# Hybrid mLSTM and short-convolution block: opening, gate arithmetic, maxima broadcast and tail in another form

## Chip, cores and metric

The kernel runs on one core of a Trainium2 chip. The metric is device time of one execution in microseconds, the median of several runs. TensorE (PE) multiplies matrices, VectorE (DVE) and ScalarE (ACT) do elementwise work, GpSimd (POOL) a little of it, SyncE (SP) issues the DMAs. Each engine runs its own instructions in order; between engines they wait on semaphores.

## The reference

One decoder layer on x (256 tokens, 2048 features), float32 throughout. What is computed:

```python
mod = silu(c) @ w_ada + b_ada                      # shift, scale, gate
h = rms_norm(x, norm1_w) * (1 + scale) + shift
proj = h @ w_in + b_in       # q k v o z | i f | u B C z_b | gA gB
h_a = mlstm(q, k, v, i, f)                         # 8 heads, running max m as stabiliser
h_a = rms_norm(sigmoid(o) * h_a, headnorm_w) * silu(z)
h_b = B * causal_conv3(C * u) * silu(z_b)
merged = sigmoid(gA) * (h_a @ w_proj_a) + sigmoid(gB) * (h_b @ w_proj_b)
out = rms_norm(x + gate * (merged @ w_out), normf_w)
```

## The kernel before

**Units.** All weights are streamed once in units of 128x1024 float32 (512 KB), in the order of the list that `units()` yields: "outer" units (q/k, v, o, z, gA: one block of 128 rows of w_in and half of a group's columns, accumulated over 16 row blocks k), two "if" units for the gates, "inner" units (gB, u, C, B, zb, yA, yB: a block j of 512 output columns, eight units each), and "out" units (w_out: row block k, half of the columns). SP loads a unit into `raw`, up to six ahead. ACT copies it into a rounded head `wh` (L302), DVE subtracts that for the remainder `wl` (L308), and TensorE multiplies three times: head by head, remainder by head, head by remainder. A unit is 12 matmuls of 512 columns or 24 of 256. The loop over UNITS first splits the unit two places ahead (`advance`), then issues this unit's matmuls, then runs one entry of the list `fillers`: the list by which everything that is not a weight matmul is dealt out between the units. The order on each engine is the order of the code.

**Opening (L127 to L280).** xT (x transposed, four DMAs) and the row c are loaded. c goes into row 0 of a zeroed tile `c_row`, and four matmuls with ones (L207) spread it over the partitions for Silu (`silu_c`, tile c_b). ACT squares xT in four pieces, DVE adds some of them, and matmuls with ones (L221) sum them over the features; the outcome stands on all partitions, 256 tokens wide, so that rstd_b is its root (L236) and reciprocal (L266) over 128x256. `keep_warm(n)` issues n matmuls on ones (L198) whose result nobody reads: `WARM[0]` at the start, `WARM[1]` behind the sums. The columns of w_ada come as pieces (part 1 scale, 0 shift, 2 gate; row block k; half) which DVE multiplies with c_b and sums (L261). After the fourth piece of block k, xT is scaled (L271) and h is made as head on ACT (L255) and remainder on DVE (L256). The first weight matmul is L333 of q/k.

**Gates.** `gates_rows` takes the i and f rows (8 heads by 256 tokens) out of PSUM beside gB block 0. `gates_math` is four fillers, `one` to `four` (L523 to L550): log-sigmoid, running sum, running maximum, and the negated maximum `mrow` as head and remainder, each 8x256. `gates_cols` (L553) turns two of the rows into columns with four transposes. Then three fillers a head follow each other (`queue_mlstm`): `stage_a` (scores, and the head's row of `mrow` spread over 128 partitions by two matmuls with 8 rows, L574 and L575), `stage_b1` to `b3` (decay matrix), `stage_c` (values), `stage_d`, and after all heads `stage_e`, `stage_y` and the transposes `stage_t`.

**Tail (from L984).** The out units accumulate into cur[t, half], t being the two tiles of 128 tokens. The split weights of the last KEEP = 4 row blocks are kept in keepH and keepL: the loop over them completes t = 0 alone, with the halves alternating, and afterwards the TAIL list completes t = 1 in six pieces of 512 or 256 columns (L1003). `out_evac` multiplies each piece by the gate (L854) and adds x (L855) on DVE, squares with a sum on ACT (L861), and multiplies by normf_w on POOL (L863). `out_root` takes the root, `out_finish` scales chunks of 512 columns (L895 on DVE, L897 on ACT; the last one, L893, with the weights on DVE) and SP sends them out.

Of the kernel before, what the change touches and what calls it, by code (L numbers as in the profile page):

```python
# [45 lines left out]
KEEP = 4  # L46
WARM = (9, 16)
# [4 lines left out]
def units():  # L52
# [43 lines left out]
def body(ctx: ExitStack, tc: tile.TileContext, wu, wa, xT_d, x_d, cols_d, rows_d, out_d):  # L96
# [32 lines left out]
    c_row = slot("s3", [128, D], "c_row")  # L129
    dve.memset(ones, 1.0)  # L130
    dve.memset(c_row[:, 0:1024], 0.0)
    pool.memset(c_row[:, 1024:2048], 0.0)
    dve.memset(dummy, 1.0)
# [9 lines left out]
    identr = slot("identr", [NH, NH], "identr", F32R)  # L143
# [3 lines left out]
    pieces = [(part, k, half) for k in range(16) for part in (1, 0) for half in range(2)]  # L147
# [60 lines left out]
    ssq = psum("a", "ssq")[:, 0, 0:S]  # L208
# [49 lines left out]
    def ada_piece(n):  # L258
# [6 lines left out]
        if n == 2:  # L265
            dve.reciprocal(rstd_b, rstd_b)  # L266
        if part == 0 and half == 1:
            a, b = ab[:, 0, k:k + 1], ab[:, 1, k:k + 1]
            dve.scalar_tensor_tensor(a, acc[:, 1, k, 0:1], bs1[:, k:k + 1], acc[:, 1, k, 1:2], op0=ALU.add, op1=ALU.add)
            dve.tensor_tensor(a, a, col("n1", k), op=ALU.mult)  # L270
            dve.scalar_tensor_tensor(xT[:, k, :], xT[:, k, :], a, rstd_b, op0=ALU.mult, op1=ALU.mult)  # L271
            dve.scalar_tensor_tensor(b, acc[:, 0, k, 0:1], col("b_shift", k), acc[:, 0, k, 1:2], op0=ALU.add, op1=ALU.add)
            blocks.append((state["now"], k))
            if k == 0:
                split_head(0, 0)
                make_h(0)
                split_head(0, 1)
# [240 lines left out]

    def gates_math():
# [557 lines left out]
```

## Time and profile before

| what | us |
|---|---|
| median of three runs | 1154.69 (1153.08 to 1155.09) |
| profiled execution, its own time | 1153.19 |
| its span, first to last instruction | 1151.4 |
| PE busy in the span | 1134.3 |
| DVE busy | 832.9 |
| ACT busy | 573.4 |

The profile is one execution. Its span is 1.8 us shorter than its time: that is what lies around the first and last instruction. The page gives busy times and the costliest groups; the timeline lists instructions in order of time, rows of equal ones merged, with the idle time before them and what ended it; the chain of waits goes back from the last instruction to what released each. A matmul's length in the timeline contains the time it takes to drain through the array, so the rate is read from starts, or from the length of a long row divided by its count.

### The profile page before, as it was taken

What the parts mean: (1) busy time and instruction counts of PE and PEld (TensorE: products, weight loads), DVE (VectorE), ACT (ScalarE), POOL (GpSimd) and SP (SyncE); (2) the same over time, 40 slices, a digit from 0 to 9 for tenths busy, and PEclk for the clock granted to TensorE, in tenths of its full rate; (3) what the DMA queues carried; (4) which work ended last, traced back from release to release, by engine and by line L of the source; (5) the groups of instructions that cost most, each with busy time, mean ns of one, the idle gap of its engine ahead of it and who ended that gap; (6) DMA issues with size and microseconds to landing.
All of it is one profiled execution on the core that took longest, in us unless ns stands there. A gap on an engine that the chain in (4) does not pass through costs nothing.

```text
span 1151.4 us, 16498 instructions
## 1 busy us (share of the span) xinstructions
PE 1134.3 (99%) x6402; PEld 1021.1 (89%) x6402; DVE 832.9 (72%) x1016; ACT 573.4 (50%) x668; POOL 16.5 (1%) x26
## 2 busy tenths in 40 slices
PE   8999999999999999999999999999999999999996
PEld 7888899988888888888999999999999888888885
DVE  6999998999888768667587666666666655555566
ACT  6764444464454546544547644544544444443453
POOL 0000000000000000000000000000000000000003
PEclk9999999999999999999999999999999999999999
DMA  9999999999888767644468676666665766487662
GB/s 345 390 387 373 338 334 348 374 376 364 319 293 312 231 217 262 201 161 151 150 190 277 189 207 206 191 210 203 194 206 194 212 197 196 145 294 234 204 201 74
DMA packets 80464, 286.41 MB, mean 249 GB/s; under 512 B 10753, under 2 KB 10881, under 8 KB 79745
## 3 DMA queue, kind: packets, MB, share of 16 engines
q1 hardware_dynamic: 80386, 285.36, 73.0%
q8 instruction: 50, 0.82, 0.3%
q14 instruction: 28, 0.23, 0.1%
HBM read 283.22 MB, written 2.11 MB: 248 GB/s over the span
## 4 chain that ended last, share of the span: by engine, by line
PE 92%; DVE 4%; ACT 2%; issue 1%; DMA 0%; DVEq 0%; SPq 0%; ACTq 0%
PE qk L333 7%; PE v L364 7%; PE z L364 7%; PE gA L364 7%; PE o L364 6%; PE out L364 6%; PE u0g L333 2%; PE C0g L333 2%; PE B0g L333 2%; PE gB1g L356 2%; PE gB2g L356 2%; PE gB3g L356 2%; PE yA3g L356 2%; PE yA0g L356 2%; PE yA2g L356 2%; PE yA1g L356 2%
## 5 line engine op out<-in xcount | busy, mean ns | idle before, releaser
L308 DVE TENSOR_TENSOR wl<-raw,wh 128x1024 fp32r<-128x1024 f32 x408 | 496.7, 1222 | 255.4 <-ACT wh L302 253.8
L302 ACT ACTIVATE wh<-raw 128x1024 fp32r<-128x1024 f32 x409 | 430.0, 1058 | 440.9 <-PE v L364 39.2
L261 DVE SCALAR_TENSOR_TENSOR ada<-ada,c_b 128x1024 f32<-128x1024 f32 x96 | 116.9, 1218 | 1.3 <-DMA ada<-wa 1.3
L364 PE MATMUL o<-wh,h 128*128 128x512 f32 x256 | 66.5, 380 | 0.6 <-DVE z L413 0.4
L364 PE MATMUL v<-wh,h 128*128 128x512 f32 x256 | 66.4, 379 | 0.0
L364 PE MATMUL z<-wh,h 128*128 128x512 f32 x256 | 66.0, 379 | 0.0
L364 PE MATMUL gA<-wh,h 128*128 128x512 f32 x256 | 66.0, 379 | 0.0
L333 PE MATMUL qk<-h,wh 128*128 128x256 f32 x512 | 62.7, 276 | 1.4 <-ACT h L255 1.4
L333 PEld LDWEIGHTS qk<-h,wh 128*128 128x128 f32 x512 | 60.0, 192 | 1.7 <-ACT h L255 1.6
L364 PEld LDWEIGHTS o<-wh,h 128*128 128x128 f32 x256 | 48.2, 189 | 8.2 <-issue 0.8
L364 PEld LDWEIGHTS v<-wh,h 128*128 128x128 f32 x256 | 48.2, 189 | 7.1 <-issue 0.4
L364 PEld LDWEIGHTS gA<-wh,h 128*128 128x128 f32 x256 | 48.4, 189 | 6.8
L364 PEld LDWEIGHTS z<-wh,h 128*128 128x128 f32 x256 | 48.3, 189 | 6.8
L364 PE MATMUL out<-wh,m 128*128 128x512 f32 x192 | 49.7, 379 | 0.0
L364 PEld LDWEIGHTS out<-wh,m 128*128 128x128 f32 x192 | 36.1, 189 | 5.1
L364 PE MATMUL v<-wl,h 128*128 128x512 f32 x128 | 38.1, 379 | 0.0
L364 PE MATMUL o<-wl,h 128*128 128x512 f32 x128 | 38.1, 379 | 0.0
L364 PE MATMUL z<-wl,h 128*128 128x512 f32 x128 | 38.1, 379 | 0.0
L364 PE MATMUL gA<-wl,h 128*128 128x512 f32 x128 | 38.1, 379 | 0.0
L333 PE MATMUL qk<-h,wl 128*128 128x256 f32 x256 | 33.8, 275 | 0.0
L333 PEld LDWEIGHTS qk<-h,wl 128*128 128x128 f32 x256 | 31.2, 192 | 0.0
L364 PE MATMUL out<-wl,m 128*128 128x512 f32 x96 | 28.6, 379 | 0.0
(430 smaller groups left out, 2114.2 us busy)
## 6 DMA issues: line engine op xcount, KB each, us to landing
raw<-wu SPq DMA_DIRECT2D x418, 512.0 KB, 4.4
ada<-wa SPq DMA_DIRECT2D x96, 512.0 KB, 6.3
xT<-xT SPq DMA_DIRECT2D x4, 512.0 KB, 6.1
gB<-rows SPq DMA_DIRECT2D x2, 1024.0 KB, 5.8
x_res<-x SPq DMA_DIRECT2D x1, 2048.0 KB, 8.0
out<-r SPq DMA_DIRECT2D x8, 256.0 KB, 2.6
gA<-rows SPq DMA_DIRECT2D x2, 512.0 KB, 7.5
z<-rows SPq DMA_DIRECT2D x2, 512.0 KB, 7.7
```

What stands on the lines that cost most here:

```text
L261: dve.scalar_tensor_tensor(t, t, 1.0, c_b[:, half * 1024:half * 1024 + 1024], op0=ALU.mult, op1=ALU.mult, accum_out=acc[:, part, k, half:h ...
L302: act.activation(head[n], r, AF.Copy)
L308: dve.tensor_tensor(rest[n], r, head[n].bitcast(F32), op=ALU.subtract)
L333: pe.matmul(o, lhsT=w[:, j + 128 * b:j + 128 * b + 128], rhs=alt(h[:, k, :]), start=st and b % 2 == 0, stop=en and b % 2 == 1, skip_group_ ...
L356: pe.matmul(o[:, t, :], lhsT=stationary(a, k, t), rhs=alt(ww[:, c0:c0 + 512]), start=st, stop=en, skip_group_check=True)
L364: pe.matmul(o[:, b, :], lhsT=stationary(a, k, t), rhs=alt(ww[:, c0 + 512 * b:c0 + 512 * b + 512]), start=st, stop=en, skip_group_check=True)
```

## The change

**Opening.** c is loaded first of all into a tile of its own, c_in, and copied into c_row, its left half by DVE and its right half by ACT. The squares are summed with tokens on the partitions: the square is the stationary operand, ones are streamed, so that `ssq` is 128x2 columns of use. Root and reciprocal work on 128x2 (`rs`). `x_norm` scales the identity by rs (two tiles dg on ACT) and spreads it with two matmuls (`rb`), which the first block's scaling reads from PSUM; ACT copies it to rstd_b for the others. The first four pieces of w_ada come as half 0 of both parts, then half 1. The warming matmuls are 6, 2, 16 and 12 in four places.

**Gates and maxima.** `gates_math` is seven fillers, and one idle filler goes, so the heads start two units later. The head and the remainder of the maxima stand in one tile of 40 partitions (0 to 7 and 32 to 39, zeros between, prepared at unit 60 by `pick_prepare`); `pick(h)` makes a 40x128 selector on ACT, and one matmul with 40 rows spreads both. One idle filler before the last transpose goes.

**Tail.** The last four row blocks of the out units come as half 0 of all four and then half 1. All splits left are issued at once behind the first of them. The first token tile's four chunks are scaled on ACT, one piece of the TAIL list earlier than before; of the second tile's chunks DVE scales 0 and 3, ACT 1 and 2, and ACT issues the DMA of chunk 2.

```diff
-WARM = (9, 16)
+WARM = (6, 2, 16, 12)
-    for k0, k1 in ((0, 4),) + tuple((k, k + 1) for k in range(4, 16)):
+    for k0, k1 in ((0, 4),) + tuple((k, k + 1) for k in range(4, 16 - KEEP)) + ((16 - KEEP, 16),):
...
+    c_in = slot("s01", [1, D], "c_in")
+    sync.dma_start(c_in, rows_d[ROWS.index("c"):ROWS.index("c") + 1, :])
...
-        if i == 0:
-            sync.dma_start(c_row[0:1, :], rows_d[ROWS.index("c"):ROWS.index("c") + 1, :])
+    dve.tensor_copy(c_row[0:1, 0:1024], c_in[:, 0:1024])
+    act.activation(c_row[0:1, 1024:2048], c_in[:, 1024:2048], AF.Copy)
...
-    pieces = [(part, k, half) for k in range(16) for part in (1, 0) for half in range(2)]
+    pieces = [(part, 0, half) for half in range(2) for part in (1, 0)]
+    pieces += [(part, k, half) for k in range(1, 16) for part in (1, 0) for half in range(2)]
...
-            pe.matmul(ssq, lhsT=ones, rhs=sq[:, b, :], start=first and b == 0, stop=last and b == n - 1)
+            for t in range(2):
+                pe.matmul(ssq[:, t, 0:128], lhsT=sq[:, b, 128 * t:128 * t + 128], rhs=ones, start=first and b == 0,
+                          stop=last and b == n - 1)
...
+    keep_warm(WARM[1])
     square(0)
+    silu_c(0)
     square(1)
-    silu_c(0)
-    dve.tensor_tensor(sqs[0], sqs[0], sqs[1], op=ALU.add)
-    dve.tensor_tensor(sqs[0][:, 0:2, :], sqs[0][:, 0:2, :], sqs[0][:, 2:4, :], op=ALU.add)
-    sum_squares(sqs[0][:, 0:2, :], True, False)
     square(2)
-    sum_squares(sqs[2], False, False)
+    dve.tensor_tensor(sqs[2][:, 0:2, :], sqs[2][:, 0:2, :], sqs[2][:, 2:4, :], op=ALU.add)
     square(3)
+    silu_c(1)
+    sum_squares(sqs[0], True, False)
+    sum_squares(sqs[1], False, False)
+    sum_squares(sqs[2][:, 0:2, :], False, False)
     sum_squares(sqs[3], False, True)
-    silu_c(1)
     act.activation(dummy, ones[:, 0:1], AF.Sqrt)
+    rs = slot("rs", [128, 2, 1], "rs")
+    act.activation(rs, ssq[:, :, 0:1], AF.Sqrt, bias=eps_c, scale=1.0 / D)
+    keep_warm(WARM[2])
...
-    act.activation(rstd_b, ssq, AF.Sqrt, bias=eps_c, scale=1.0 / D)
-    act.activation(identr, ident[0:NH, 0:NH], AF.Copy)
-    keep_warm(WARM[1])
+    def x_norm():
+        dve.reciprocal(rs, rs)
+        for t in range(2):
+            dg = wp.tile([128, 128], F32, name=f"dg{t}", tag="dmat", bufs=2)
+            act.activation(dg, ident, AF.Copy, scale=rs[:, t, :])
+            pe.matmul(rb[:, 0, 128 * t:128 * t + 128], lhsT=ones, rhs=dg, start=(t == 0), stop=(t == 1),
+                      skip_group_check=True)
+        keep_warm(WARM[3])
...
         if n == 2:
-            dve.reciprocal(rstd_b, rstd_b)
+            x_norm()
+            scale()
+            split_head(0, 0)
+            split_head(0, 1)
...
+    def pick(h):
+        ml["pick", h] = wp.tile([32 + NH, 128], F32R, name=f"pick{h}", tag="pick", bufs=2)
+        act.activation(ml["pick", h], ones[0:32 + NH, :], AF.Copy, scale=ml["sel"][:, h:h + 1])
...
-        return [one, two, three, four]
+        return [one, two, three, four, five, six, seven]
...
-        pick = identr[:, h:h + 1].to_broadcast([NH, 128])
-        pe.matmul(p[:, 1, 0:256], lhsT=pick, rhs=ml["mr"][0], start=True, stop=False)
-        pe.matmul(p[:, 1, 0:256], lhsT=pick, rhs=ml["mr"][1], start=False, stop=True)
+        pe.matmul(p[:, 1, 0:256], lhsT=ml["pick", h], rhs=ml["mr"], start=True, stop=True)
...
-        fillers.extend([idle, idle, gates_cols])
+        fillers.extend([idle, gates_cols])
...
-            fillers.append(heads((stage_b2, i - 1), (stage_d, i - 3), (stage_b3, i - 1)))
+            fillers.append(heads((stage_b2, i - 1), (stage_d, i - 3), (stage_b3, i - 1), (pick, i + 1)))
...
-            elif c % 2 == 0:
+            elif t and c == 0:
                 dve.tensor_scalar(r, r, tot, None, op0=ALU.mult)
             else:
                 act.activation(r, r, AF.Copy, scale=tot)
-            sync.dma_start(out_d[128 * t:128 * t + 128, cs], r)
+            (act if t and c == 2 else sync).dma_start(out_d[128 * t:128 * t + 128, cs], r)
...
-        advance(n + HD)
+        advance(NU - 1 if n >= NU - 2 * KEEP + 1 else n + HD)
...
-        elif (lo, n) in TAIL[2:4]:
-            out_finish(0, (0, 1) if (lo, n) == TAIL[2] else (2, 3))
+        elif (lo, n) in TAIL[1:3]:
+            out_finish(0, (0, 1) if (lo, n) == TAIL[1] else (2, 3))
...
-    out_finish(1, (0, 2, 1, 3))
+    out_finish(1, (0, 1, 3, 2))
```

ACT from the program's start to the root, before; sq are the squares, c_b the Silu of c, and in brackets stands what an instruction waits for (DMAHW: a DMA, PE, DVE, Pool: that engine):

```order
L193 ACT_TABLE_LOAD
L193 ACTIVATE dummy<-dummy 128x1 [waits DVE_49]
L212 ACTIVATE sq_119<-xT 128x1024 [waits DMAHW0_49]
L212 ACTIVATE sq_120<-xT 128x1024 [waits DMAHW2_49]
L215 ACTIVATE c_b<-c_112 128x1024 [waits PE_49]
L212 ACTIVATE sq_121<-xT 128x1024 [waits DMAHW3_49]
L212 ACTIVATE sq_122<-xT 128x1024 [waits DMAHW4_49]
L215 ACTIVATE c_b<-c_115 128x1024 [waits PE_49]
L234 ACT_TABLE_LOAD
L234 ACTIVATE dummy<-ones 128x1 [waits Activation_49]
L236 ACTIVATE rstd_b<-ssq,eps_c 128x256 [waits DVE_49,PE_49]
```

and in the changed kernel, where c_in is the loaded row:

```order
L140 ACT_TABLE_LOAD [waits DMAHW0_49]
L140 ACTIVATE c_row<-c_in 1x1024 [waits Pool_49]
L195 ACT_TABLE_LOAD
L195 ACTIVATE dummy<-dummy 128x1 [waits DVE_49]
L214 ACTIVATE sq_118<-xT 128x1024 [waits DMAHW1_49]
L217 ACTIVATE c_b<-c_111 128x1024 [waits PE_49]
L214 ACTIVATE sq_119<-xT 128x1024 [waits DMAHW2_49]
L214 ACTIVATE sq_120<-xT 128x1024 [waits DMAHW3_49]
L214 ACTIVATE sq_121<-xT 128x1024 [waits DMAHW4_49]
L217 ACTIVATE c_b<-c_114 128x1024 [waits PE_49]
L239 ACT_TABLE_LOAD
L239 ACTIVATE dummy<-ones 128x1 [waits Activation_49]
```

A copy with a table load of its own now stands first, the load waits for a DMA, and a second load follows ahead of Silu.

TensorE from the program's start to the first weight matmul, before:

```order
L198 MATMUL warm<-ones 128x128 x9
L207 MATMUL c_112<-c_row,ones 128x512 x2
L207 MATMUL c_115<-c_row,ones 128x512 x2
L221 MATMUL ssq<-sq_119,ones 128x256 x2
L221 MATMUL ssq<-sq_121,ones 128x256 x4
L221 MATMUL ssq<-sq_122,ones 128x256 x4
L198 MATMUL warm<-ones 128x128 x16
```

and in the changed kernel (numbers of matmul calls at the end; rb are the two that spread the reciprocal):

```order
L200 MATMUL warm<-ones 128x128 x6
L209 MATMUL c_111<-c_row,ones 128x512 x2
L209 MATMUL c_114<-c_row,ones 128x512 x2
L200 MATMUL warm<-ones 128x128 x2
L224 MATMUL ssq<-ones,sq_118 128x128 x8
L224 MATMUL ssq<-ones,sq_119 128x128 x8
L224 MATMUL ssq<-ones,sq_120 128x128 x4
L224 MATMUL ssq<-ones,sq_121 128x128 x8
L200 MATMUL warm<-ones 128x128 x16
L252 MATMUL rb<-dg_200,ones 128x128
L252 MATMUL rb<-dg_203,ones 128x128
L200 MATMUL warm<-ones 128x128 x12
```

The sums' ten calls of 256 columns are 28 of 128, and calls on ones stand on both sides of rb.

DVE beside gB block 0, in the second half of the gate arithmetic; wl are the weight remainders that TensorE needs unit by unit, before:

```order
L532 TENSOR_TENSOR gate_rows<-gate_rows 8x256
L533 RECIPROCAL gate_rows<-gate_rows 8x256
L308 TENSOR_TENSOR wl_4129<-raw_3993,wh_4128 128x1024
L536 TENSOR_TENSOR gate_rows<-gate_rows 8x256
L537 TENSOR_TENSOR gate_rows<-gate_rows 8x256
L538 SCALAR_TENSOR_TENSOR gate_rows<-gate_rows 8x256
L539 MEMSET gate_rows 8x256
L540 SCALAR_TENSOR_TENSOR gate_rows<-gate_rows 8x256
L308 TENSOR_TENSOR wl_4152<-raw_4016,wh_4151 128x1024
L543 TENSOR_TENSOR gate_rows<-gate_rows 8x256
L544 SCALAR_TENSOR_TENSOR gate_rows<-gate_rows 8x256
L545 TENSOR_SCALAR gate_rows<-gate_rows 8x256
```

and in the changed kernel:

```order
L571 TENSOR_TENSOR gate_rows<-gate_rows 8x256
L333 TENSOR_TENSOR wl_4171<-raw_4036,wh_4170 128x1024
L574 RECIPROCAL gate_rows<-gate_rows 8x256
L333 TENSOR_TENSOR wl_4190<-raw_4059,wh_4189 128x1024
L577 TENSOR_TENSOR gate_rows<-gate_rows 8x256
L578 TENSOR_TENSOR gate_rows<-gate_rows 8x256
L579 SCALAR_TENSOR_TENSOR gate_rows<-gate_rows 8x256
L333 TENSOR_TENSOR wl_4211<-raw_4083,wh_4210 128x1024
L582 MEMSET gate_rows 8x256
L583 SCALAR_TENSOR_TENSOR gate_rows<-gate_rows 8x256
L584 TENSOR_TENSOR gate_rows<-gate_rows 8x256
L333 TENSOR_TENSOR wl_4232<-raw_4109,wh_4231 128x1024
```

The reciprocal and the later operations are dealt out so that one to three of them stand between two remainders, where four or five stood.

## Rows read from the trace of the kernel before

**Rows 1.** The page, part 1: engine, busy us (share of the span), instructions.
```profile
PE 1134.3 (99%) x6402; PEld 1021.1 (89%) x6402; DVE 832.9 (72%) x1016; ACT 573.4 (50%) x668; POOL 16.5 (1%) x26
```

**Rows 2.** Chain of waits: start, length in us, what, matmul instructions.
```profile
42.64 15.54 PE z L364 x72
...
151.41 80.56 PE qk L333 x720
```

**Rows 3.** Timeline, opening: start and length us, engine, line, operation, tiles [idle before].
```profile
0.80 0.38 SPq L136 DMA_DIRECT2D xT<-xT  x1
...
1.12 3.86 PE L198 MATMUL warm<-ones 128*128 128x128 f32 x18 [1.12 <-DVE ones L130]
...
2.23 0.31 SPq L138 DMA_DIRECT2D c_row<-rows  x1
...
5.68 3.67 PE L207 MATMUL c<-c_row,ones 128*128 128x512 f32 x8 [0.71 <-DMA c_row<-rows]
...
10.13 1.99 ACT L212 ACTIVATE sq<-xT 128x1024 f32<-128x1024 f32 x2
...
13.05 1.28 ACT L234 ACT_TABLE_LOAD   x1
...
15.78 3.73 PE L198 MATMUL warm<-ones 128*128 128x128 f32 x32
...
16.49 1.75 DVE L266 RECIPROCAL rstd_b<-rstd_b 128x256 f32<-128x256 f32 x1 [0.15 <-ACT rstd_b L236]
...
19.69 0.49 DVE L271 SCALAR_TENSOR_TENSOR xT<-xT,ab,rstd_b 128x256 f32<-128x256 f32 x1
...
20.90 2.12 PE L333 MATMUL qk<-h,wh 128*128 128x256 f32 x16 [1.38 <-ACT h L255]
```

**Rows 4.** Timeline, the eight units of gB block 0 (443 to 467 us).
```profile
443.45 1.03 PE L356 MATMUL gB0g<-wh,h 128*128 128x512 f32 x4
...
449.39 1.28 ACT L526 ACT_TABLE_LOAD   x1 [1.97 <-DVE gate_rows L525]
...
450.68 0.42 ACT L526 ACTIVATE gate_rows<-gate_rows 8x256 f32<-8x256 f32 x1
...
454.19 1.73 DVE L533 RECIPROCAL gate_rows<-gate_rows 8x256 f32<-8x256 f32 x1
...
459.13 1.19 DVE L308 TENSOR_TENSOR wl<-raw,wh 128x1024 fp32r<-128x1024 f32 x1
...
466.66 1.13 PE L356 MATMUL gB1g<-wh,h 128*128 128x512 f32 x4
```

**Rows 5.** Timeline, PE at the scores of head 0 (475 us).
```profile
474.96 0.39 PE L572 MATMUL sc<-qk 128*128 128x128 f32 x2
...
475.28 0.38 PE L574 MATMUL sc<-mrow,identr 8*128 8x256 f32 x1
...
475.50 0.28 PE L575 MATMUL sc<-mrow,identr 8*128 8x256 f32 x1
...
475.71 1.13 PE L356 MATMUL gB1g<-wh,h 128*128 128x512 f32 x4
```

**Rows 6.** Timeline, the tail (1128 us to the end).
```profile
1128.77 0.69 DVE L854 TENSOR_TENSOR r<-out,gate_b 128x512 f32<-128x512 f32 x1 [5.40 <-PE out L364]
...
1129.86 0.38 PE L1003 MATMUL out<-keepH,m 128*128 128x512 f32 x1
...
1139.87 1.24 DVE L895 TENSOR_SCALAR r<-r,tot 128x512 f32<-128x512 f32 x1
...
1140.14 0.71 ACT L897 ACTIVATE r<-r,tot 128x512 f32<-128x512 f32 x1
...
1141.49 0.38 PE L1003 MATMUL out<-keepH,m 128*128 128x256 f32 x1 [1.24 <-DVE r L854]
...
1143.26 0.42 DVE L854 TENSOR_TENSOR r<-out,gate_b 128x256 f32<-128x256 f32 x1
...
1146.29 0.75 DVE L893 SCALAR_TENSOR_TENSOR r<-r,tot,nf 128x512 f32<-128x512 f32 x1
```

More of the change, by code (lines that the diff above doesn't have):

```diff
@@ L129, in body @@
     c_row = slot("s3", [128, D], "c_row")
+    c_in = slot("s01", [1, D], "c_in")
+    sync.dma_start(c_in, rows_d[ROWS.index("c"):ROWS.index("c") + 1, :])
     dve.memset(ones, 1.0)
+    dve.memset(dummy, 1.0)
     dve.memset(c_row[:, 0:1024], 0.0)
     pool.memset(c_row[:, 1024:2048], 0.0)
-    dve.memset(dummy, 1.0)
     dve.memset(eps_c, EPS)
@@ L264, in ada_piece, with scale @@
             dve.tensor_scalar(bs1, cols[:, COL["b_scale"]:COL["b_scale"] + 16], 1.0, None, op0=ALU.add)
-        if n == 2:
-            dve.reciprocal(rstd_b, rstd_b)
-        if part == 0 and half == 1:
-            a, b = ab[:, 0, k:k + 1], ab[:, 1, k:k + 1]
+        a, b = ab[:, 0, k:k + 1], ab[:, 1, k:k + 1]
+        def scale():
             dve.scalar_tensor_tensor(a, acc[:, 1, k, 0:1], bs1[:, k:k + 1], acc[:, 1, k, 1:2], op0=ALU.add, op1=ALU.add)
             dve.tensor_tensor(a, a, col("n1", k), op=ALU.mult)
-            dve.scalar_tensor_tensor(xT[:, k, :], xT[:, k, :], a, rstd_b, op0=ALU.mult, op1=ALU.mult)
+        if n == 2:
+            x_norm()
+            scale()
+            split_head(0, 0)
+            split_head(0, 1)
+        if part == 0 and half == 1:
+            if k:
+                scale()
+            dve.scalar_tensor_tensor(xT[:, k, :], xT[:, k, :], a, rstd_b if k else rb[:, 0, 0:S], op0=ALU.mult,
+                                     op1=ALU.mult)
             dve.scalar_tensor_tensor(b, acc[:, 0, k, 0:1], col("b_shift", k), acc[:, 0, k, 1:2], op0=ALU.add, op1=ALU.add)
@@ L517, in gates_rows, with pick_prepare @@
         fillers.extendleft([row(0), row(1)])
+    def pick_prepare():
+        sel = slot("sel", [32 + NH, NH], "sel")
+        dve.tensor_tensor(sel, ident[0:32 + NH, 0:NH], ident[0:32 + NH, 32:32 + NH], op=ALU.add)
+        ml["sel"] = sel
+        ml["mr"] = slot("mrow", [32 + NH, S], "mrow", F32R)
+        for t in range(2):
+            act.activation(ml["mr"][:, 128 * t:128 * t + 128], ones[0:32 + NH, :], AF.Copy, scale=0.0)
+    def pick(h):
+        ml["pick", h] = wp.tile([32 + NH, 128], F32R, name=f"pick{h}", tag="pick", bufs=2)
+        act.activation(ml["pick", h], ones[0:32 + NH, :], AF.Copy, scale=ml["sel"][:, h:h + 1])
     def gates_math():
@@ L532, in two, with three, four @@
             dve.tensor_tensor(r[6], r[3], r[6], op=ALU.subtract)
+        def three():
             dve.reciprocal(r[7], r[4])
-        def three():
+        def four():
             dve.tensor_tensor(r[6], r[6], r[7], op=ALU.mult)
@@ L538, in three, with five, six, seven @@
             dve.scalar_tensor_tensor(r[1], r[1], 0.0, r[5], op0=ALU.min, op1=ALU.subtract)
+        def five():
             dve.memset(r[2], 0.0)
             dve.tensor_tensor_scan(r[3], r[1], r[2], 0.0, op0=ALU.add, op1=ALU.add)
-        def four():
             dve.tensor_tensor(r[0], r[0], r[3], op=ALU.subtract)
+        def six():
             dve.tensor_tensor_scan(r[4], r[0], r[0], 0.0, op0=ALU.max, op1=ALU.max)
             dve.tensor_scalar(r[5], r[4], -1.0, None, op0=ALU.mult)
-            mr = slot("mrow", [NH, 2, S], "mrow", F32R)
-            ml["mr"] = mr[:, 0, :], mr[:, 1, :]
-            act.activation(mr[:, 0, :], r[5], AF.Copy)
-            dve.tensor_tensor(mr[:, 1, :], r[5], mr[:, 0, :].bitcast(F32), op=ALU.subtract)
+            act.activation(ml["mr"][0:NH, :], r[5], AF.Copy)
+        def seven():
             dve.scalar_tensor_tensor(r[6], r[3], -1.0, r[4], op0=ALU.mult, op1=ALU.subtract)
-        return [one, two, three, four]
+            dve.tensor_tensor(ml["mr"][32:32 + NH, :], r[5], ml["mr"][0:NH, :].bitcast(F32), op=ALU.subtract)
+        return [one, two, three, four, five, six, seven]
     def gates_cols():
         R = ml["R"]
+        pick(0)
         pt = psum("a", "gates_t")
@@ L686, in yt @@
             return lambda: stage_t(i)
-        fillers.extend([y2(0), y2(2), yt(0), y2(4), yt(1), y2(6), yt(2), idle, yt(3)])
+        fillers.extend([y2(0), y2(2), yt(0), y2(4), yt(1), y2(6), yt(2), yt(3)])
     def operands(grp):
@@ L912, in body @@
         state["now"] = n
-        advance(n + HD)
+        if n == 60:
+            fillers.append(pick_prepare)
+        advance(NU - 1 if n >= NU - 2 * KEEP + 1 else n + HD)
         while blocks and (blocks[0][0] < n or kind == "outer" and blocks[0][1] <= k):
@@ L999, in body @@
         for k in range(16 - KEEP, 16):
-            u = NU - 2 * (16 - k) + half
+            u = NU + k - 16 - KEEP * (1 - half)
             for a, w in ((hb["mH"], head[u]), (hb["mH"], rest[u]), (hb["mL"], head[u])):
```

7 lines of the change are left out of this document (3 added, 4 removed).

## Prediction

> **What bounds the kernel now.** I read the page's busy times first: TensorE is busy 99% of the span [rows 1]. The chain of waits then shows it running for tens of microseconds without a break, at 15.54/72 = 0.216 us for a matmul of 512 columns and 80.56/720 = 0.112 us for one of 256 [rows 2]. DVE, ACT and DMA matter only where TensorE stops or runs work that isn't a weight matmul. There are four such places, and I read the timeline at each: the opening up to the first weight matmul at 20.90 [rows 3], the gate arithmetic beside gB block 0 [rows 4], the maxima's broadcast once a head [rows 5], and the tail from 1128.77 [rows 6]. The rest of the kernel's matmuls are the same in number and size after the change, so the sum is made over these four.
>
> **Opening.** What goes: the 1.75 us reciprocal over 128x256 and its wait [rows 3]; DVE's sum over two squares. What comes: the c row arrives alone and first, DVE and ACT copy it into c_row, TensorE sums squares with tokens on the partitions, a reciprocal over 128x2 replaces the long one, two diagonal matmuls (rb) spread it, and 12 warming matmuls stand between rb and the first weight matmul.
> The new order has a catch on ACT: its first instruction is now the table load for the copy, and it carries the copy's wait for the c DMA. The trace shows such a load waiting: at 449.39 one starts only when DVE's gate_rows is there, lasts 1.28 us, and its ACTIVATE follows at 450.68 [rows 4]. Behind the copy stands a second load, for Silu. All five squares and Silus that the sum needs queue behind both.
> When is c there? SP's first issue is at 0.80. The c row issued at 2.23 released TensorE at 5.68, 3.45 us later and behind an xT transfer [rows 3]; at most that, so 4.25. Nothing stands ahead of it now; I take 3.6, and 3.0 as the early end (estimates, off that one row). Then ACT: load 1.28 (as at 13.05), copy about 1.0 (two 128x1024 in 1.99, [rows 3]), load 1.28, dummy 0.2: 7.35. Square, Silu, three squares at 1.0 each: 12.3. TensorE's sums for the last square come behind sq 2, which DVE first adds (0.7): 8 records of 0.112 from 12.0, then 16: 14.7. (One call on fp32 operands is two records: 16 warm calls gave 32 in 3.73 [rows 3].) Then the row of calls that nothing can shorten: 16 warm, 32 x 0.112 = 3.6, to 18.3; rb 0.45, to 18.7; 12 warm, 24 x 0.112 = 2.7, to 21.4. The other path, rb to xT scaling to h, needs 20.90 - 19.69 = 1.21 us [rows 3] and about 0.3 to read PSUM: 20.2, so it is covered by the warming matmuls. The first weight matmul is at 21.4 against 20.90: +0.5. The first two units gain 0.2, since the first DVE remainders are then ready beforehand. Opening: **+0.3**. Bounds: if the load does not hold the queue and c is early, -1.3. The other way, the first 18 warm records took 3.86 us, 0.214 each and twice the later 0.112 [rows 3]; there are 12 now, and if the rate rises late, part of the sums' 56 records run at 0.214 as well: with c late (+0.65) together +2.0.
> The Trainium skill, "ScalarE: Activation LUTs", section "What ACT_TABLE_LOAD costs", puts a drain of about 1.38 us behind each 1.28 us load. The ACTIVATE at 450.68, 0.01 us behind its load, shows no such drain [rows 4]; by the page the two loads would add 2.8 us here and the sum below would end at 1151.9. The sum goes by the row.
>
> **Gates.** The eight units of gB block 0 take 466.66 - 443.45 = 23.2 us; at 12 matmuls of 0.216 each they need 20.7 [rows 2, 4]. Of the 2.5 between I give 0.5 to four small transposes that stand there (an estimate), so 2.0 us is stall: DVE stands 1.73 us in a reciprocal [rows 4], in the same part as four shorter operations, then in two more long parts, each above the 2.59 - 1.2 = 1.4 us that a unit leaves beside its weight remainder (1.19, [rows 4]), and TensorE waits for remainders and, behind them, for ACT. In seven parts, six fit into 1.4 us. The reciprocal part exceeds it by 0.3, and the seventh (0.8) falls into the unit that also evacuates gB block 0 (1.2): 1.2 + 1.2 + 0.8 = 3.2 against 2.59, 0.6 over, with some 0.1 of slack. I keep 0.5 of the stall plus its restart: **-1.4**. Bounds -2.0 (all hidden) and -0.2 (ACT's copy of the maxima, which waits for DVE in part six, holds up the next weight split as now). The heads start two units later. That delays the last transposes by one unit and puts one convolution part (1.3 us on DVE) into a later unit, where nothing on TensorE waits for it by the timeline: nothing.
>
> **Maxima.** After the last score matmul TensorE is free at 474.96 + 2 x 0.11 = 475.18, and the next weight matmul starts at 475.71: 0.53 us for two matmuls of eight rows, the second 0.22 behind the first [rows 5]. One of them goes: 8 x 0.22 = **-1.8**. Whether the surrounding delay stays isn't shown for 40 rows. If it goes too, 8 x (0.53 - 0.11) = -3.4; if one matmul costs as much as one and a half of the old, -0.9. The 8 picks (40x128 on ACT) are made a loop earlier, on an engine that is busy half the time [rows 1].
> The Trainium skill, "TensorEngine Tiling (Array Packing)", "Key Properties", says that changing the tiling mode drains TensorE. Eight rows and forty rows are both another mode than 128, so by it only the matmul's own 0.22 goes, which is the value taken; without it the end of -3.4 would hold.
>
> **Tail.** TensorE enters the second token tile at 1129.86 [rows 6]. It needs 24 x 0.216 + 48 x 0.112 = 10.6 us, to 1140.4, plus some 0.35 to DVE's last product: 1140.75. That product starts at 1143.26 now, because DVE is behind: TensorE waits 1.24 us at 1141.49 for a DVE product, which stood behind a 1.24 us scaling of the first tile [rows 6]. After the change the first tile's left half ends 3 units (3 x 6 x 0.216 = 3.9 us) earlier, so two products and two sums (4 x 0.69 = 2.8) are done before the rush, and the two of the first tile's four scalings that DVE has leave it (1.24 and more). That is 4 us off DVE, more than the 2.5 us by which it is late, so TensorE becomes the bound: **-2.5** at the last product, and the sum, the square and ACT's root follow it as now. Cover: ACT takes four scalings of 0.71 [rows 6] between squares; it has room until the last square, and if it hasn't, up to 1.3 comes back. The last outputs: DVE scales one chunk less, its 0.75 us product [rows 6] starts 0.45 earlier, and ACT issues the last DMA. The four transfers still share the DMA engines: **-0.2**. The tail is -2.7; bounds -1.2 and -3.3. [...]
>
> **Sum.** +0.3 - 1.4 - 1.8 - 2.7 = -5.6. The profiled execution took 1153.19 (span 1151.4), so 1147.6. It lies 1.5 below the median of the three timed runs, 1154.69; I predict medians: 1154.69 - 5.6 = **1149.1**.
>
> **Rivals.**
> (a) The opening gains as well: the copy's load doesn't hold ACT. -1.3 in place of +0.3: 1147.5. For it: DMA and sums are all earlier. Against it: the load at 449.39 did wait.
> (b) Gains are only part: TensorE keeps the gate stall (-0.2), ACT's scalings hold the tail (-1.2), the opening pays 2.0, the maxima give 0.9: 1154.4, no change. It needs all four bad ends at once; three of them give 1152 to 1153.
> (c) Each of the two table loads keeps ACT for about as long again as it lasts (2 x 1.28 = +2.6): 1151.7. Against it: 0.01 us between load and ACTIVATE at 450.68 [rows 4]. This is the page's drain in the kernel's own numbers.
> (d) The picks end up in TensorE's way: pick(i+1) stands on ACT behind the copy of the head's scores, which waits for DVE, and if it comes late TensorE waits at each of 8 heads. From 5.6/8 = 0.7 us a head on the kernel is slower than before; at 1.1 us it is 8 x 1.1 - 5.6 = +3.2: 1157.9. Against it: a pick is asked for a whole three-unit round (7.8 us) ahead.
> (e) The new order doesn't do what it says in the tail, because DVE still starts the left half late behind the weight remainders: -0.2 in place of -2.7, 1151.6. Against it: DVE is idle 5.40 us ahead of 1128.77 [rows 6].
>
> **How the numbers follow.** Forecast 0.57, (a) 0.14, (b) 0.12, (c) 0.04, (d) 0.05, (e) 0.08. A difference of 0.2% (2.3 us) is about the least that a measurement of this kernel can tell. Forecast, (a), (c) and (e) are faster by more: 0.83; (b) is the same: 0.12; (d) is slower: 0.05. For the range I add the bounds half-way (all four rarely go one way) and 0.8 for the runs' own spread: 1146.0 to 1152.8 leaves out (b), (d) and a little of (a).
>
> **What would show it.** First qk matmul near 21.4, preceded by warming matmuls without a gap (a gap there, or a start below 20.5, speaks against the opening's sum). Two table loads ahead of the first square, the first starting when c lands. In gB block 0, about 21.8 us from first to last. At each head some 0.3 us between scores and weights in place of 0.53. In the tail, TensorE without a wait above 0.3, the last product near 10.9 us behind its first matmul of the second tile, and ACT busy between squares. The prediction is wrong if TensorE waits in a stretch where it doesn't now, above all between the heads.

## The result and the profile after

The changed kernel takes 1148.14 us (median of 4 runs, 1147.75 to 1148.29); beside it the kernel before took 1153.88 (4 runs, 1152.54 to 1155.09). The ratio is 0.9942, with a 95% interval of 0.9929 to 0.9955: faster by about 0.6%, where 1149.1 was predicted. The profiled execution took 1148.13 us with a span of 1146.4, so against the one of before (1153.19, span 1151.4) the span is 5.0 shorter.

The page, part 1, of the kernel after (answers to [rows 1]): TensorE's busy time is 2.3 us more in a span that is 5.0 us shorter.

```profile
PE 1136.6 (99%) x6456; PEld 1025.7 (89%) x6456; DVE 829.9 (72%) x1014; ACT 580.6 (51%) x685; POOL 15.3 (1%) x26
```

The same milestones on TensorE's timeline in both traces say where the 5.0 us came from. Each line is the start of the first matmul of that group; the last column is what the stretch up to it added to the difference.

| first matmul of | before | after | after - before | added in the stretch |
|---|---|---|---|---|
| qk (first weights) | 20.90 | 21.49 | +0.59 | +0.59 |
| gB block 0 | 443.45 | 443.96 | +0.50 | -0.09 |
| zb block 0, behind gates and heads | 615.60 | 613.14 | -2.45 | -2.96 |
| the second token tile's tail | 1129.86 | 1127.41 | -2.45 | 0.00 |
| last matmul of the tail | 1142.82 | 1138.10 | -4.72 | -2.27 |
| end of the span | 1151.40 | 1146.41 | -4.99 | -0.27 |

Between gB block 0 and zb block 0, TensorE's time from one start to the next, summed over the matmuls of each kind, splits the 2.96: the 96 matmuls of gB block 0 take 2.14 less, and the heads' maxima 0.92 less (16 matmuls with 3.41 us before, 8 with 2.49 after). Everything else there is equal to about 0.1.

**Opening**, timeline of the kernel after (answers to [rows 3]):

```profile
0.80 0.35 SPq L131 DMA_DIRECT2D c_in<-rows  x1
...
2.45 1.28 ACT L140 ACT_TABLE_LOAD   x1 [2.45 <-DMA c_in<-rows]
...
3.74 1.05 ACT L140 ACTIVATE c_row<-c_in 1x1024 f32<-1x1024 f32 x1
3.84 4.50 PE L209 MATMUL c<-c_row,ones 128*128 128x512 f32 x8
...
4.81 1.28 ACT L195 ACT_TABLE_LOAD   x1
...
6.22 1.04 ACT L214 ACTIVATE sq<-xT 128x1024 f32<-128x1024 f32 x1
...
8.62 6.42 PE L224 MATMUL ssq<-ones,sq 128*128 128x128 f32 x56
...
14.87 3.74 PE L200 MATMUL warm<-ones 128*128 128x128 f32 x32
...
18.44 0.61 PE L252 MATMUL rb<-dg,ones 128*128 128x128 f32 x4
18.89 2.84 PE L200 MATMUL warm<-ones 128*128 128x128 f32 x24
...
21.49 1.25 PE L358 MATMUL qk<-h,wh 128*128 128x256 f32 x9
```

From 3.84 to 21.49 each group of matmuls starts where the one ahead ends: the opening is now one unbroken queue on TensorE, and its length sets when the first weights start. The first table load waited for the row of c, as predicted, but c was there at 2.45, only 1.65 us after its issue.

**Gates**, the gB block 0 matmuls of the kernel after (operation, count, min/median/max length in ns, first and last start), then rows of the timeline (answers to [rows 4]):

```profile
L381 PE MATMUL gB0g<-wh,h x64: 379/379/382, 444.0 to 464.0; 128*128 128x512 f32 x64
L381 PE MATMUL gB0g<-wl,h x32: 379/379/379, 444.8 to 464.5; 128*128 128x512 f32 x32
```
```profile
456.58 1.73 DVE L574 RECIPROCAL gate_rows<-gate_rows 8x256 f32<-8x256 f32 x1
...
458.24 1.15 DVE L333 TENSOR_TENSOR wl<-raw,wh 128x1024 fp32r<-128x1024 f32 x1
...
460.36 0.59 PE L381 MATMUL gB0g<-wl,h 128*128 128x512 f32 x2
```

The block is at full pace, 464.68 - 443.96 = 20.72 us. The remainder wl behind the reciprocal ends at 459.39, 0.97 us before the matmul at 460.36 reads it.

**Heads**, TensorE and its weight loads (PEld) at the scores of head 0, kernel after (answers to [rows 5]):

```profile
478.60 0.38 PE L616 MATMUL sc<-qk 128*128 128x128 f32 x2
478.92 0.38 PE L617 MATMUL sc<-mrow,pick 40*128 40x256 f32 x1
479.23 1.13 PE L381 MATMUL gB1g<-wh,h 128*128 128x512 f32 x4
```
```profile
478.91 0.18 PEld L617 LDWEIGHTS sc<-mrow,pick 40*128 40x128 f32 x1
479.23 0.73 PEld L381 LDWEIGHTS gB1g<-wh,h 128*128 128x128 f32 x4
```

From the last score matmul (478.60 + 2 x 0.11) to the weights at 479.23 is 0.41 us, not the 0.3 I had said. The one matmul of 40 rows takes 0.31 us up to the weights (478.92 to 479.23), where the second of the old pair took 0.21 (475.50 to 475.71 [rows 5]).

**Tail**, kernel after (answers to [rows 6]):

```profile
1127.41 0.38 PE L1047 MATMUL out<-keepH,m 128*128 128x512 f32 x1
...
1135.15 0.65 PE L1047 MATMUL out<-keepH,m 128*128 128x256 f32 x2
...
1138.41 0.43 DVE L896 TENSOR_TENSOR r<-out,gate_b 128x256 f32<-128x256 f32 x1
...
1140.98 0.74 DVE L935 SCALAR_TENSOR_TENSOR r<-r,tot,nf 128x512 f32<-128x512 f32 x1
...
1141.92 0.41 ACTq L940 DMA_DIRECT2D out<-r  x1
```

One pause of 0.17 us is left on TensorE (between the two matmuls of the row at 1135.15, a wait for a DVE product). The last product starts 11.00 us behind the first matmul of the tile; it was 13.40.

### The profile page after: what moved, and what is told of

It is laid out like the page before. It is cut to its first block, busy times and chain, and to the rows that moved or that the text cites. A ratio compares the mean times of both kernels' runs of the same rounds, so it can differ in the third digit from the quotient of the medians.

```text
span 1146.4 us, 16619 instructions
## 1 busy us (share of the span) xinstructions
PE 1136.6 (99%) x6456; PEld 1025.7 (89%) x6456; DVE 829.9 (72%) x1014; ACT 580.6 (51%) x685; POOL 15.3 (1%) x26
## 4 chain that ended last, share of the span: by engine, by line
PE 97%; ACT 1%; DVE 1%; issue 1%; ACTq 0%
PE gA L389 7%; PE qk L358 7%; PE v L389 7%; PE z L389 7%; PE o L389 7%; PE out L389 6%; PE u0g L358 2%; PE B0g L358 2%; PE C0g L358 2%; PE gB2g L381 2%; PE gB3g L381 2%; PE gB1g L381 2%; PE yA3g L381 2%; PE yA2g L381 2%; PE yA1g L381 2%; PE yA0g L381 2%
```

## Experiments

Each number is a median with its lowest and highest run; where the place matters, I add what the trace shows. "The changed kernel" is the one above, 1148.14.

**1. One part undone at a time.** The first takes back the opening (its six pieces of the diff), the other three one part each:

```diff
# old_gates
-        return [one, two, three, four, five, six, seven]     # parts merged
+        return [one, two, three, four]
...
-        fillers.extend([idle, gates_cols])
+        fillers.extend([idle, idle, gates_cols])
...
# old_maxima
...
-        pe.matmul(p[:, 1, 0:256], lhsT=ml["pick", h], rhs=ml["mr"], start=True, stop=True)
+        pe.matmul(p[:, 1, 0:256], lhsT=pick, rhs=ml["mr"][:, 0, :], start=True, stop=False)
+        pe.matmul(p[:, 1, 0:256], lhsT=pick, rhs=ml["mr"][:, 1, :], start=False, stop=True)
...
# old_tail
...
-        advance(NU - 1 if n >= NU - 2 * KEEP + 1 else n + HD)
+        advance(n + HD)
...
-        elif (lo, n) in TAIL[1:3]:
+        elif (lo, n) in TAIL[2:4]:
...
```

Gates as before:

> The changed kernel with the gate math in four parts and two idle slots again, all else changed. Theory: the parts are the whole of it, the first gate block (gB0g, 96 matmuls) goes back from 20.7 to about 23.2 us with its waits behind the reciprocal's part, so 2.0 to 2.4 us more than the changed kernel, about 1150.3. By the term on record (1.4, a stall of 0.5 kept) it would be about 1149.5. Rival: the stall in the kernel before came from where the opening's schedule put the transfers, not from the parts: then less than 0.5 more.

Measured 1150.60 (7 runs, 1149.73 to 1151.25), 2.5 more. In the trace the block takes 23.21 us again: its weight matmuls take 2.15 more from start to start, and the four transposes that fall into it again 0.34. The rows of this kernel show the wait that the seven parts remove:

```profile
459.87 1.19 DVE L333 TENSOR_TENSOR wl<-raw,wh 128x1024 fp32r<-128x1024 f32 x1
...
461.11 0.70 PE L381 MATMUL gB0g<-wl,h 128*128 128x512 f32 x2 [0.36 <-DVE wl L333]
```

Behind it stands a second wait, of 0.76 us, for ScalarE, whose split of the next units waits in its queue behind the copy of the maxima. The parts, together with the idle fillers that move with them, are the cause, and the theory's size holds; my term on record was too small.

Maxima as before:

> The changed kernel with the maxima spread by two 8-row matmuls a head again, all else changed (no picks are built). By the rows of the two traces the pair takes 0.43 us a head and the single 40-row one 0.31, since the weight load of a matmul with another row count does not go ahead of the matmul before it: 8 x 0.115 = 0.9 us more than the changed kernel, about 1149.0. By the term on record (8 x 0.22) it would be 1.8 more, 1149.9. If the picks on ScalarE had a cost of their own, this one would be up to 0.5 less than these.

Measured 1148.94 (5 runs, 1148.30 to 1149.87), 0.8 more; these runs only just clear the changed kernel's (up to 1148.29), so the size rests on the trace. By it the stretch of gates and heads takes 0.90 more, all of it in the pair of matmuls (3.41 against 2.49 us). The 0.9 holds, the 1.8 falls.

Tail as before:

> The changed kernel with the order of the last units, the order of the last finishing steps and the split of the outputs as before, all else changed. Theory: TensorE waits again about 2.3 us between the last tiles (rows of 0.3 to 1.4 us before the products), the last product comes 13.4 us behind the first matmul of the second tile instead of 11.0, and the end is about 0.2 longer: 2.5 more than the changed kernel, about 1150.6. Rival: half of the gain came from the whole kernel being earlier against the transfers of the last weights, then 1.2 or less.

Measured 1150.48 (6 runs, 1150.13 to 1151.09), 2.3 more. In the trace the tail's matmuls take 2.28 and the end 0.14 more, and the waits of TensorE list what is back (us in all, times, the longest):

```profile
PE out L1047 <- DVE r L896: 1.6, 2, 1.2
```

The opening as before:

> The changed kernel with the opening of the kernel before (its WARM, its row c, its sums of squares, its order of the first pieces); gates, maxima and tail stay changed. Theory from the two traces: the new opening costs 0.5 to 0.6 us, because TensorE's queue (56 passes of sums, then 32 warming passes, the broadcast, 24 more) sets the start; so this one begins its weights at 20.9 instead of 21.49 and takes about 0.5 us less than the changed kernel, 1147.6. Rival: the opening's later start is an accident of one execution or is given back at the stall near 38 us, then the time is the changed kernel's within 0.2; or the opening gains as in my case of faster openings, then this one is slower by up to 1.5.

Measured 1148.40 (5 runs, 1147.88 to 1150.17): by the medians no difference that can be told, with three runs at 1147.9 to 1148.4 (mean granted clock 0.998 or 0.999) and two at 1149.5 and 1150.2 (0.996). The profiled one is of the two. Its first weights start at 21.27, 0.2 before the changed kernel's, but its first 24 weight matmuls take 1.7 us longer. Busy time by stretch (start:end, length, PE, PEld, DVE, ACT, POOL, granted clock, DMA share, GB/s):

```profile
19.00:22.00 3.00, 0.81 (x6) 0.73 (x6) 2.32 (x8) 1.29 (x3) 0.00 (x0) 1.00 1.02 412
22.00:26.00 4.00, 4.00 (x23) 4.00 (x23) 4.00 (x5) 2.43 (x3) 0.00 (x0) 0.57 1.03 414
```

TensorE stood idle for 2.19 us ahead of its first weights, and then the granted clock fell from 1.0 to 0.5 (2.4 to 1.2 GHz): 0.57 over 4 us is 3.4 us at 0.5. The 12 warming matmuls behind the broadcast fill this gap, which my sum had not counted (experiment 4 asks what that is worth). This became a second theory: a part of the gain is in executions of the kernel before that lose the clock here.

**2. That theory, on the kernel before.** Only its second WARM number is changed, so that the warming matmuls reach further towards the first weights:

```diff
-WARM = (9, 16)
+WARM = (9, 22)
```

> The kernel before with 22 instead of 16 warming matmuls ahead of its first weights, so that TensorE has no gap there (15.78 + 22 x 0.233 = 20.9). Theory: the kernel before has in most executions a fall of the granted clock behind this gap (one profiled run with the old opening shows it at 22.3 to 25.7 us; its own profiled execution does not), and that is the 0.7 us by which the medians differ by more than the spans: with the gap closed the times lie within 0.8 us of each other around 1153.2. Rival: the spread of the kernel before, 1153 to 1157 us, is elsewhere: then the median is that of the kernel before or up to 0.3 later, with the same spread.

Measured 1153.23 (11 runs: nine at 1152.7 to 1153.95, one at 1154.95 and one at 1155.8), against 1155.01 for the kernel before beside it (15 runs, 1153.08 to 1157.06). The ratio over all of these runs is 0.9990, interval 0.9981 to 0.9999. Of the 15 runs of the kernel before, four lie at 1153.1 to 1153.6 with a mean granted clock of 0.998 or 0.999 and eleven at 1154.8 to 1157.1 with 0.995 to 0.997. The 21 runs of the kernel before beside experiments 1, 3 and 4 keep this order but fill the space between (up to 1154.06 at 0.998 or more, from 1154.13 at 0.997 or less), so there are not two clear groups. The longer warming moves the median to the early runs. That fits the theory; it is not complete, since two runs are still late and the nine lie within 1.2 us and not 0.8, and in the profiled one 0.84 us without matmuls are left (h came at 21.67). No late run of the kernel before was profiled, so where it loses its clock is not shown; and one fall like that of old_opening costs 1.7 us, while the latest runs lie 4 us above the best.

**3. What the price of a head is.** The pick and the maxima are padded with zero rows to 128 rows, so that the matmul has its neighbours' row count:

```diff
-        sel = slot("sel", [32 + NH, NH], "sel")
+        sel = slot("sel", [128, NH], "sel")
...
-        ml["mr"] = slot("mrow", [32 + NH, S], "mrow", F32R)
+        ml["mr"] = slot("mrow", [128, S], "mrow", F32R)
...
-        ml["pick", h] = wp.tile([32 + NH, 128], F32R, name=f"pick{h}", tag="pick", bufs=2)
+        ml["pick", h] = wp.tile([128, 128], F32R, name=f"pick{h}", tag="pick", bufs=2)
...
```

> The changed kernel, but the pick and the maxima rows are padded with zeros to 128 rows, so the one matmul a head has the row count of its neighbours. Theory (the price is the change of row count: the weight load does not go ahead, 0.1 us on the way in, 0.1 on the way out): the start-to-start time of this matmul falls from 0.311 to 0.11 us and that of the 128-column matmul ahead of it from 0.205 to 0.11, together 0.19 to 0.3 a head, 1.5 to 2.4 us less than the changed kernel, about 1146.2. Rival: the price is the type of the operands or the wait for the pick, not the rows: then no difference, 1148.1.

Measured 1145.48 (5 runs, 1144.58 to 1145.83; ratio to the kernel before 0.9912, 0.9897 to 0.9927), 2.7 less than the changed kernel. TensorE's stretch of gates and heads is 3.14 us shorter, 0.39 a head, more than the 0.19 to 0.3 expected. Head 0 of this kernel, matmuls and loads:

```profile
478.29 0.39 PE L616 MATMUL sc<-qk 128*128 128x128 f32 x2
478.43 0.36 PE L617 MATMUL sc<-mrow,pick 128*128 128x256 f32 x1
478.63 1.02 PE L381 MATMUL gB1g<-wh,h 128*128 128x512 f32 x4
```
```profile
478.40 0.19 PEld L617 LDWEIGHTS sc<-mrow,pick 128*128 128x128 f32 x1
478.51 0.74 PEld L381 LDWEIGHTS gB1g<-wh,h 128*128 128x128 f32 x4
```

Now the weights' load starts at 478.51, 0.12 ahead of its matmul at 478.63; with 40 rows the load and its matmul both start at 479.23. The two score matmuls also run closer together (0.17 us less a head), and the weight matmuls behind lose 0.11 us a head that they had spent waiting for a load. So most of what such a matmul costs here is the change of row count, on both sides.

**4. The warming matmuls of the opening.** Only the numbers in WARM change:

```diff
-WARM = (6, 2, 16, 12)
+WARM = (6, 2, 16, 0)    # warm_last_0
+WARM = (6, 2, 4, 0)     # warm_4_0
+WARM = (6, 2, 4, 8)     # warm_4_8
```

> The changed kernel without the 12 warming matmuls behind the broadcast (WARM 6, 2, 16, 0). Theory: the first weights begin when the first block of h stands, at about 20.3 instead of 21.49, and the later work moves with them: 1.2 us less, 1147.0, as long as the granted clock stays at 1.0 through the 1.2 us without matmuls. Rival 1: the clock falls behind that gap, as it did at 22.3 us in the profiled run with the old opening (2.2 us without matmuls, then 3.4 us at 0.5, about 1.7 us lost): 1148.6. Rival 2: the transfers are what the second block waits for, so that the stall near 38 us grows by what the start gains: 1148.1.

> The changed kernel with 4 warming matmuls between the sums and the broadcast instead of 16, and none behind it (WARM 6, 2, 4, 0). Theory: the broadcast then follows the second scaled identity at 16.3, xT the fourth piece at 17.0, and the first weights begin at about 18.3, 3.2 us less, 1145.0, if the clock holds. Rival 1: the clock falls behind the gaps (0.5 and 1.5 us without matmuls), 1.7 us lost: 1146.6. Rival 2: the stall near 38 us takes back what is over about 1 us: 1147.

> The changed kernel with 4 warming matmuls between the sums and the broadcast instead of 16, and 8 behind it instead of 12 (WARM 6, 2, 4, 8). Theory: TensorE is busy almost without a gap and the first weights begin at 18.7 instead of 21.49: 2.7 us less, 1145.4, with a clock that does not fall. Rival: transfers take it back at the stall near 38 us: 1147 or more. Against the run without any behind the broadcast it tells whether the clock needs them.

Measured 1147.06 (1146.41 to 1147.57), 1145.51 (1144.85 to 1146.27) and 1146.11 (1145.82 to 1146.29). The first weights start at 20.35, 18.08 and 18.68, and the clock did not fall in any of the three profiles, although TensorE stood idle for 1.25 us ahead of the weights in the first and 1.24 in the second. So in the changed opening the 12 matmuls behind the broadcast cost 1.1 us, and no trace shows what they save. The start holds to 0.2 us as expected, and so does what the first run brings (1.1). The two others give 0.65 and 0.86 us back at one place, in their rows near 35 us. Those of warm_4_0:

```profile
34.14 1.22 DVE L278 SCALAR_TENSOR_TENSOR ada<-ada,c_b 128x1024 f32<-128x1024 f32 x1
...
34.33 0.64 PE L389 MATMUL o<-wl,h 128*128 128x512 f32 x2
...
35.28 0.48 DVE L273 SCALAR_TENSOR_TENSOR h<-xT,ab,h 128x256 fp32r<-128x256 f32 x1
...
35.81 1.13 PE L389 MATMUL o<-wh,h 128*128 128x512 f32 x4 [0.84 <-DVE h L273]
```

It is not transfers that hold TensorE here: the remainder of the second block of h stands on DVE behind a product of 1.22 us.

**5. Does a table load hold the opening?** ScalarE loads its Silu table at once, and both halves of the row of c are copied on DVE:

```diff
+    act.activation(dummy, dummy, AF.Silu)
     dve.tensor_copy(c_row[0:1, 0:1024], c_in[:, 0:1024])
-    act.activation(c_row[0:1, 1024:2048], c_in[:, 1024:2048], AF.Copy)
+    dve.tensor_copy(c_row[0:1, 1024:2048], c_in[:, 1024:2048])
...
-    act.activation(dummy, dummy, AF.Silu)
```

> The changed kernel, but ScalarE loads its Silu table before the row of c is there, and VectorE copies both halves of the row, so that no table load waits for the transfer and there is one load less ahead of the squares. Theory (TensorE's queue sets the start: the row's matmuls at half clock, then 56 passes of sums back to back): the squares come some 0.9 us earlier and nothing else does; first weights at 21.3 to 21.7, 1148.1. Rival (the table loads that wait for c hold the opening, as one case of the prediction had it): the first weights begin 0.9 to 1.3 us earlier, 1147.0.

Measured 1148.09 (5 runs, 1147.71 to 1149.07): no difference. The first square starts 0.85 us earlier than in the changed kernel, the sums do not:

```profile
3.84 5.19 PE L209 MATMUL c<-c_row,ones 128*128 128x512 f32 x8
...
5.37 1.06 ACT L214 ACTIVATE sq<-xT 128x1024 f32<-128x1024 f32 x1 [3.08 <-DMA xT<-xT]
...
9.31 6.42 PE L224 MATMUL ssq<-ones,sq 128*128 128x128 f32 x56
```

The matmuls that spread c took 5.19 us here and 4.50 in the changed kernel's profile, and the first weights start at 22.18 and 21.49: the same 0.69 apart. In the runs that keep this queue (old_maxima 5.26 and 22.25, old_gates 4.71 and 21.70, pick128 4.18 and 21.17) the first weights always start 16.99 us plus the length of this group. Within it one matmul follows another after 0.85 us at first and after 0.43 later, half pace and then full; the change comes at 5.0 us in pick128's trace, at 5.6 in the changed kernel's and at 7.2 in old_maxima's, where the trace's record of a clock granted at 1.0 (2.4 GHz) begins. How early the clock rises sets the start of the whole kernel; ScalarE does not.

**6. Both gains together.** The 128-row picks with WARM (6, 2, 4, 0); the second kernel has in addition the block of h right behind the split of the next unit:

```diff
                 split(n)
                 state["w"] = n + 1
+                while blocks:
+                    make_h(blocks[0][1])
...
```

> The changed kernel with the 128-row picks and with WARM (6, 2, 4, 0). Theory: the two gains are in different stages and add: 3.1 and 2.6 less, 1142.4. Rival: without warming matmuls the clock falls in some executions behind the 1.2 us gap (1.7 lost there): a median up to 1144.

> The run before it in this call, and a block of h is made right behind the split of the next unit instead of behind the whole step, so that VectorE's remainder of h stands ahead of a product of 1.2 us in its queue. Theory: the stall near 35 us (1.0 us longer than the usual step, TensorE waiting for the remainder of h) goes: 0.9 less, 1141.5. Rival: VectorE or ScalarE then waits in order for the other at each of 15 blocks and later units are split later: 1142.4 or more.

Measured 1141.72 (4 runs, 1141.60 to 1142.79; ratio 0.9889, 0.9876 to 0.9903) and 1141.36 (4 runs, 1141.14 to 1142.36; ratio 0.9886, 0.9872 to 0.9899), a further 6.4 and 6.8 us below the changed kernel. The two gains add (2.7 and 2.6 by medians); the 1.1 us that the first has over their sum isn't explained, since its three faster runs have no trace. In both profiled executions the clock fell behind the gap ahead of the first weights; busy time by stretch of the first:

```profile
18.00:20.00 2.00, 2.00 (x12) 2.00 (x12) 2.00 (x3) 0.92 (x2) 0.00 (x0) 0.53 1.05 414
20.00:22.00 2.00, 2.00 (x13) 2.00 (x13) 2.00 (x4) 1.13 (x2) 0.00 (x0) 0.62 1.00 397
```

That cost 1.65 us, and this execution is the slowest of its four. The gap was 1.33 us; 1.24 us in warm_4_0 had no such fall. What decides between them isn't settled here. The step of h does what was expected: in the second kernel the remainder starts at 34.69, ahead of the product, and the pause is gone.

```profile
34.24 0.59 PE L391 MATMUL o<-wl,h 128*128 128x512 f32 x2
...
34.67 1.03 PE L391 MATMUL o<-wh,h 128*128 128x512 f32 x4
34.69 0.48 DVE L273 SCALAR_TENSOR_TENSOR h<-xT,ab,h 128x256 fp32r<-128x256 f32 x1
35.09 1.22 DVE L278 SCALAR_TENSOR_TENSOR ada<-ada,c_b 128x1024 f32<-128x1024 f32 x1
```

Between the two spans it brings 0.46 us, between the medians 0.36; the 0.9 expected was too much. In the profiled pair that is because behind the clock's fall the pause was 0.4 us and not the 1.0 of warm_4_0; why the medians, of runs without a trace, differ by no more stays open.

## Why the prediction was right, and where its steps were off

The sign, three of the four causes and the total were right: -5.6 on record, -5.0 from profile to profile, -5.7 between the medians. The terms were less good than the sum: gates and maxima missed by 0.7 and 0.9 in opposite directions, and that they cancel is luck. So is a part of the agreement with the medians, which hold 0.7 us that no term of the sum stands for (see "The base").

| term | on record | bounds on record | trace | run with that part undone |
|---|---|---|---|---|
| opening, up to gB block 0 | +0.3 | -1.3 to +2.0 | +0.50 | no difference by medians |
| gates | -1.4 | -2.0 to -0.2 | -2.14 | +2.5 (2.15 in the trace) |
| maxima | -1.8 | -3.4 to -0.9 | -0.92 | +0.8 (0.90 in the trace) |
| tail | -2.7 | -3.3 to -1.2 | -2.54 | +2.3 (2.42 in the trace) |
| sum | -5.6 | | -5.1 (spans: -5.0) | |

- **Opening.** The end was right (21.4 on record, 21.49), by the argument that counted: the warming matmuls and the broadcast are a row that nothing shortens. What led up to it was partly wrong. I let ScalarE's last square release the sums; the sums ran from 8.62 without a pause for 6.42 us, so TensorE's own queue was the pace. I also had c at 3.6 us, and it came at 2.45. With ScalarE alone moved, the start does not move with it (experiment 5). The two mistakes cancelled, which is luck: earlier c, but half of the clock's rate in the matmuls that spread it. Nor is the +0.5 a measured price: it compares one execution of each, while the first weights start at 21.17 to 22.25 in the profiles that have this queue and at 20.90, 21.27 and 21.67 in the three with the old one (before, old_opening, before_warm22). By the medians the opening is worth nothing that can be told.
- **Gates.** The mechanism was right, the term mis-sized, and the outcome beyond its bound of -2.0: "I keep 0.5 of the stall". None is left. I charged the part with the reciprocal (0.3 over) and the seventh (0.6 over) as if they had 0.1 us of slack, but the split of a unit is made two units ahead, and the remainder behind the reciprocal is still 0.97 us early. The rest of the 2.5 that the block lost, 0.34 us, is the four transposes: they only moved to the next block. I had put them at 0.5.
- **Maxima.** The mechanism was half right: "One of them goes: 8 x 0.22". The 0.22 from the first of the pair to the second did go, but the one that stays takes 0.31 us up to the weights where the second took 0.21, so only 0.115 a head went: 8 x 0.115 = 0.92. My lower bound of 0.9 just held it. I had weighed the Trainium skill, "TensorEngine Tiling (Array Packing)", section "Key Properties", for the statement that a mode switch drains; the trace fits it (the load behind 40 rows starts only at 479.23, 0.31 us behind the matmul at 478.92), and the delay around the pair did stay. But I took what stays to be unchanged, and it grew from 0.21 to 0.31; how that divides into stream, load and drain isn't shown. The Trainium skill, "TensorE: Matmul & The Clock Gate", section "Step-by-step: what each phase is for", says that the queue pulls weight loads ahead of matmuls in flight where the row groups don't conflict or the load goes to the spare weight buffer. Among equal row counts the trace agrees (0.12 us ahead in pick128); across a change of row count no load here goes ahead, and there the measurement decides.
- **Tail.** Right in mechanism and size: last product 11.00 us behind (10.9 on record), one wait of 0.17 where none above 0.3 was expected, the end 0.27 shorter (0.2 on record). ScalarE's issue of one transfer lasts 0.41 us, and nothing waits for it.
- **The base.** The step "I predict medians: 1154.69 - 5.6" took for granted that the 1.5 us by which the median of before lies above its profiled execution would still be there after the change. After, the four runs lie within 0.54 us and the profiled one, 1148.13, lies at the median. Two things therefore meet in the 1.0 us by which the forecast was too high: the sum was 0.5 too good against the profiles, and the base 1.5 too high. What went is, as far as experiment 2 and old_opening tell, the fall of the clock in the kernel before; in the medians beside the result it is worth 0.7 us. Beside the experiments the kernel before had higher medians (1154.63, 1155.54 and 1155.01 of 12, 9 and 15 runs): by these the change gains 6.5 to 7.4 us, 1.4 to 2.3 more than the profiles show. I had read one profile of before, without such a fall, and took the spread for noise.
- **Rivals.** (a) falls: experiment 5 gives ScalarE its table early and nothing follows. (b), (d) and (e) fall by the terms above; TensorE does not wait between the heads. (c) falls: the activations begin 0.01 us behind their loads (2.45 + 1.28, the copy of c at 3.74). The Trainium skill, "ScalarE: Activation LUTs", section "What ACT_TABLE_LOAD costs", has a drain of about 1.38 us there; no load in this trace shows it.

## What to carry to other kernels

Here a matmul of 40 rows between matmuls of 128 rows cost mostly the two changes of row count: padding it with zeros to 128 rows gave back 0.39 us a head, where having one instead of two gave 0.115. So try the padding before counting how many there are. When the median lies well above the profiled execution, look for what the profile does not show (here probably a gap on TensorE behind which the clock falls in most executions) and ask whether the change touches it. Arithmetic that shares an engine with a feed needed only to be cut into parts that fit between two feeds plus what is made ahead, not into parts that fit one unit exactly.

## What the runs showed of the hardware that I had not expected

- A 40-row matmul among 128-row ones costs 0.39 us a head more than the same matmul padded to 128 rows: 0.11 itself, 0.17 on the score matmuls ahead of it and 0.11 on the weight matmuls behind it.
- Most executions of the kernel before (11 of 15 in experiment 2) run 1.7 to 4.0 us longer than its best, at a mean granted clock of 0.995 to 0.997 in place of 0.998 to 0.999. In the three profiles that show a fall (old_opening, combo, combo_h; none is of the kernel before) the clock goes to 0.5 for 3.4 us shortly after a gap of 2.19, 1.33 and 1.43 us, which costs 1.65 to 1.7 us; gaps of 1.24 us (warm_4_0), 1.25 us (warm_last_0) and 1.38 us [rows 3] were followed by none in theirs.
- At the start the clock rises at a different time in each execution, and the first weights move with it, from 21.17 to 22.25 us in the five profiled executions of the changed opening (the result's, old_gates, old_maxima, old_tail, pick128); there the record of the clock at 1.0 begins at 5.0 to 7.2 us.
- A row of 8 KB issued first was there 1.65 us after its issue; issued behind a 512 KB transfer it released TensorE 3.45 us after [rows 3].
